# Cache pages in visits of four with seven buffers, and the prompt's causal mask added in VectorE's pass

## The chip, the cores and the metric

The kernel runs on one core of a Trainium2 chip. The metric is the device time of one launch in microseconds, as the median of several runs. The profile shows one such execution, instruction by instruction; its span runs from the first to the last instruction.

## The reference

One inference step of a two-layer decoder: a 512-token prompt and 8 decoding samples of 8 tokens (64 tokens, 576 columns with the prompt's), model width 1024, all in float32. Layer 0 is a gated DeltaNet mixer. Then keys and values are computed once, and layer 1 is a differential attention over them: 8 heads, each with two score components of 64 and values of 128. The prompt attends causally to itself; each sample attends to 1024 cached tokens, in 8 pages of 128 tokens found by a page table, and to its own 8 tokens.

```python
def diff_block(q, k, v, q_pos, k_pos, lam):
    s = jnp.einsum('bqhmd,bkhmd->bhmqk', q, k) * DIFF_DH ** -0.5
    s = jnp.where((k_pos[None, :] <= q_pos[:, None])[None, None, None], s, -jnp.inf)
    p = jax.nn.softmax(s, axis=-1)
    p = p[:, :, 0] - lam * p[:, :, 1]
    return jnp.einsum('bhqk,bkhe->bqhe', p, v)

k_past = cache_k[page_table].reshape(db, past, DIFF_HEADS, 2 * DIFF_DH)
v_past = cache_v[page_table].reshape(db, past, DIFF_HEADS, DIFF_VH)
...
o = rms_norm(o, sub_gain) * (1.0 - lam_init)
o = o * jax.nn.silu(z).reshape(b, L, DIFF_HEADS, DIFF_VH)
return o.reshape(b, L, DIFF_WIDTH) @ w_out
```

## The kernel before

The first part (`phase_a`, to about 640 us) does layer 0. The change lies in the second, `phase_b`. Its order of instructions is not written by hand: a small planner, the class `Second`, runs many generators. Each yields a step: an engine (E is TensorE, A ScalarE, D and S VectorE, P and Q POOL, None a step on no engine), an assumed cost in microseconds, and conditions: results that must be done and rooms (buffers) that must be free. At each turn the planner takes the step that can start first, and of those with the same start the lowest rank. It prices a change of TensorE's tiling itself:

```python
        if mode != self.mode:
            self.cost += 0.2 if mode == (128, 128) else 0.115
```

`pin` then fixes that order on TensorE, ScalarE, VectorE, POOL and SP, so each engine runs its list strictly in order and waits where an input is late. On the chip the waits are by data, not by the planner's clock.

The generators that matter here:

- `weights` and `split_w` load 47 weight sets (128 x 8 x 128, 512 KB each) through two raw buffers on SP's queue. ScalarE casts a set to `whi` (L2018), and POOL, for some sets VectorE, subtracts to get `wlo` in two pieces (L2024). The matrices come in rows of eight sets: the first layer's output projection, then from set 8 queries, from 16 keys, from 24 values, from 32 the gate z, from 40 the output projection. Up to set 23 four buffers turn; from 24 on the room `w2`, with two buffers early and a third (`P.third`) from about 870 us, when the memory of the earlier stage is free. Set 26 has a place of its own.
- `second_projections` (rank 1000, so whatever else can start goes first) multiplies these sets with the hidden state, split in the same way: `run_part` issues three matmuls of 288 columns for each of 8 chunks, 24 for one half of a set. In `out_second`, at the end, four half-tiles of sets 40 and 41 run up to their last chunk before they are finished.
- `Pages.loads` (rank 9) loads the 128 cache pages of 512 KB, in the order keys of samples 0 to 2, then values and keys in turn. It waits for a room `pg` (five buffers), copies the page number on POOL (L2478), reads it into a register on SP (L2481) and issues the load on SP (L2483).
- `Sample2.keys` multiplies the queries with two pages at a time, in the 128x32 tiling (tile `px`); `softmax` follows, and `values` takes two value pages at a time (tile `po`). I call each such group of matmuls a visit. On the chip the pages' buffers are freed as the last matmul on them is done.
- `samples_end` gathers the samples' outputs, normalizes them and multiplies them with the gate; the samples' half of the output projection waits for that.
- `Prompt2.heads` issues the prompt's scores for each head and block of 128 queries (two components in the 64x128 tiling, into rooms `sc`), and then adds the causal mask on the diagonal block by one matmul with the identity for each (bf16, `cmaskb`). `unit` follows with the negated maximum on VectorE (L2714), the exponential on ScalarE (L2718), the combination of the two components on VectorE (L2731), TensorE's transposes into `pt2`, a copy on ScalarE (L2743) and the product with the values (`pv`).

Of the kernel before, what the change touches and what calls it, by code (L numbers as in the profile page):

```python
# [10 lines left out]
F32 = mybir.dt.float32  # L11
# [879 lines left out]
HELD = 4  # L891
EV = 3
CH = 3
PB = 3
# [1100 lines left out]
def weights(W, K, first, n, slot):  # L1995


    for j in range(first, first + n):
        room = "w" if j < 24 else "wx" if j == 26 and EV > 2 else "w2"
        yield None, 0, Room("raw")  # L2000
        rr, = W.took
        raw = K.wraw.tile([128, 8, 128], F32, name="wraw")
        K.nc.sync.dma_start(out=raw[:], in_=K.wall[K.worder[K.wnext + j]].rearrange("p (k m) -> p k m", m=128))
        if j <= 2:
            W.done[("raw", j)] = 0.0, None
        else:
            W.load("S", 1.5, "raw", j)
        W.add(4, split_w(W, K, j, raw, rr, room, slot[room]))


def split_w(W, K, j, raw, rr, room, slot):
    nc = K.nc
    yield "A", act(1024), ("raw", j), Room(room), *((("wa", j - 1),) if j - 1 in W.sets and j > 1 else ())
    took, = W.took
    phi, plo = slot(took[1])
    hi = phi.tile([128, 8, 128], F32R, name="whi")
    lo = plo.tile([128, 8, 128], F32R, name="wlo")
    nc.scalar.copy(out=hi[:], in_=raw[:])  # L2018
    W.sets[j] = hi, lo, took
    W.set("wa", j)  # L2020
    for q in range(0, 8, 4):
        shared = q and HALF[0] <= j < HALF[1]
        yield ("S", dve(512)) if shared else ("P", pool_op(512))
        (nc.vector if shared else nc.gpsimd).tensor_sub(out=lo[:, q:q + 4], in0=raw[:, q:q + 4], in1=hi[:, q:q + 4].bitcast(F32))  # L2024
    W.leave(rr)
    W.set("w", j)
# [320 lines left out]
def second_projections(W, K):  # L2347
# [40 lines left out]
    for i, (m, half) in enumerate(order):  # L2388
        if i < 3:
            bank = early[i][2]  # L2390
            yield from run_part(W, K, m, bank[0], half, (6, 7), conds=heads_in)
        else:
            yield from one(m, m, half, "o", nothing)
            bank = W.done_bank
        if half:
            W.leave(W.sets[m][2])
# [19 lines left out]
    for t, bank in zip(tiles, banks):  # L2416
        W.add(0, t.evac(1, bank))
        W.leave(W.sets[8 + t.h][2])
    yield None, 0, *[("ada", n, "used") for n in range(0, len(KTS2), 2)]
# [16 lines left out]
def tile_row(W, K, tiles, j, kind, conds, first=0):  # L2436
# [6 lines left out]
    for t, half in order:  # L2443
        name = "pp" if kind in "qk" or t.h < EV and kind == "v" else "pq"
        if kind == "v" and t.h == EV and half == 0:
            yield None, 0, ("late",)
        yield from take(W, K, pick(W, "pq", "pt2", "sc", "pv") if kind == "z" and ("pv", 7, 3) in W.done else name)
        bank, = W.out
        yield from run_part(W, K, j + t.h, bank[0], half, range(8), conds=conds[half])
        W.add(0, t.evac(half, bank))  # L2450
        if half:
            W.leave(W.sets[j + t.h][2])
            if j + t.h in (20, 21, 22):
                W.leave(("w2", j + t.h - 20) if j + t.h < 22 else ("wx", 0))
        if t.h == 7:
            W.set(kind + "p", half)


class Pages:


    def __init__(self, W, K):
        self.W, self.K = W, K
        self.tiles = {}
        self.order = [("k", b) for b in range(PB)]
        for b in range(NB):
            self.order += [("v", b)] + ([("k", b + PB)] if b + PB < NB else [])

    def loads(self):
        W, K, P = self.W, self.K, self.W.P  # L2470
        nc = K.nc
        for kind, b in self.order:
            for pg in range(NPG):
                yield "Q", 0.2, Room("pg"), ("ptt",), ("sq", *PAGES_AT)
                i = b * NPG + pg
                t = K.pg.tile([128, 8, 128], F32, name="pg")
                e = t[0:1, 0, 0:1].bitcast(I32)
# [5 lines left out]
                nc.sync.dma_start(out=t[:], in_=cache[bass.ds(r, 1)].rearrange("a p (h t) -> p (a h) t", h=8))  # L2483
                W.load("S", 1.55, kind + "page", i)


class Sample2:
# [5 lines left out]
    def keys(self):  # L2493
# [14 lines left out]
        for half in range(2):  # L2508
            for pair in range(2):
                ids = [b * NPG + 4 * half + 2 * pair + i for i in range(2)]  # L2510
                yield "E", None, *[("kpage", i) for i in ids], *((Room("px"),) if pair == 0 else ())
# [3 lines left out]
                for n, i in enumerate(ids):  # L2515
                    kp, kr = self.G.tiles["k", i]
                    o = 128 * (2 * pair + n)
                    for hh in range(2):
# [64 lines left out]
    def values(self):  # L2583
        W, K, P, b = self.W, self.K, self.W.P, self.b
        nc = K.nc
        for pair in range(4):
            ids = [b * NPG + 2 * pair + i for i in range(2)]
            yield "E", None, *[("vpage", i) for i in ids], *((Room("po"),) if pair == 0 else ())
# [3 lines left out]
            for n, i in enumerate(ids):  # L2592
                vp, vr = self.G.tiles["v", i]
                pg = 2 * pair + n
                for hf in range(2):
# [21 lines left out]
def samples_end(W, K):  # L2617
# [13 lines left out]
    r0, = W.took  # L2631
    sq = K.pg.tile([128, 8, 128], F32, name="pg")[:].rearrange("p a b -> p (a b)")[:, 0:512]
    nc.scalar.activation(out=sq.rearrange("p (h t) -> p h t", t=64), in_=o, func=AF.Square)
# [40 lines left out]
class Prompt2:  # L2674
# [5 lines left out]
    def heads(self):  # L2680
        W, K, P = self.W, self.K, self.W.P
        nc = K.nc
        for h in range(8):
            for qts in (0, 1), (2,), (3,):
# [4 lines left out]
                for qt, pss in units:  # L2689
                    for m in range(2):  # L2690
                        r = slice(64 * m, 64 * m + 64)
                        W.matmul(out=pss[m], lhsT=P.qT[r, h, 128 * qt:128 * qt + 128], rhs=P.kT[r, h, 0:128 * (qt + 1)],
                                 start=(qt == qts[0]), stop=False, tile_position=(64 * m, 0))
                for qt, pss in units:
                    for m in range(2):
                        W.matmul(out=pss[m][:, 128 * qt:128 * qt + 128], lhsT=K.identb, rhs=K.cmaskb, start=False,
                                 stop=(qt == qts[-1]))
                for qt, pss in units:
                    W.add(W.rank - 1, self.unit(h, qt, pss, rooms))

    def unit(self, h, qt, pss, rooms):
# [4 lines left out]
        for m in range(2):  # L2706
# [7 lines left out]
            nc.vector.tensor_reduce(out=mx[:, m:m + 1], in_=pss[m], axis=AX.X, op=ALU.max, negate=True)  # L2714
# [3 lines left out]
            nc.scalar.activation(out=p[:, :w], in_=pss[m], func=AF.Exp, bias=mx[:, m:m + 1],  # L2718
                                 accum_out=ls[:, qt, m:m + 1])
# [69 lines left out]
def out_second(W, K):  # L2789
# [40 lines left out]
    for (m, half), bank in zip(order[:HELD], held):  # L2830
        yield from run_part(W, K, 40 + m, bank[0], half, (7,), conds=conds(half))
        W.add(0, evac(m, half, bank))
        if half:
            W.leave(W.sets[40 + m][2])
    for i, (m, half) in enumerate(order[HELD:]):
# [5 lines left out]
        if half:  # L2841
            W.leave(W.sets[40 + m][2])

# [48 lines left out]
def set_up(W, K, one):  # L2892
# [47 lines left out]
    yield "D", 0.8, ("cm",)  # L2940
    nc.vector.tensor_copy(out=K.identb, in_=K.ident)
    nc.vector.tensor_copy(out=K.cmaskb, in_=cm)
    yield "D", 0.6
# [19 lines left out]
def phase_b(K, ctx, past):  # L2963
# [16 lines left out]
    P.rstd = K.pg.tile([128, 8, 128], F32, name="pg")[:].rearrange("p a b -> p (a b)")[:, 0:NT]  # L2980
    K.identb = first.tile([128, 128], BF16, name="identb")[:]
    K.cmaskb = first.tile([128, 128], BF16, name="cmaskb")[:]
    P.kT = first.tile([128, 8, NT], F32, name="kT")
# [16 lines left out]
    for name, bufs in (("pp", 3), ("pt", 2), ("px", 2), ("po", 1), ("pg", PG), ("scr", SB), ("ch", CH), ("vch", EV), ("tk", 2), ("raw", 2),  # L3000
                       ("w", 4), ("w2", 3), ("wx", 1), ("qs", 2), ("p", PB), ("pTs", 1), ("os", 1), ("C", 2), ("ls", 2), ("mx", 2),
                       ("pq", 1), ("pt2", 1), ("sc", 2), ("pv", 1), ("pm0", PM[0]), ("pm1", PM[1]), ("pts", 1)):
        W.room(name, bufs)
    W.taken["pg"] = W.taken["w"] = 1
    W.taken["w2"], W.taken["wx"] = 3, 1
    W.sets[0] = *K.wq.pop(0), ("w", 0)
    W.done[("w", 0)] = max(0.0, past.done[("w", past.last)][0] - past.free["E"]), None
    own = K.whi, K.wlo
    pages = Pages(W, K)
# [3 lines left out]
    slot = {"w": lambda i: own if i % 4 < 2 else qx, "w2": lambda i: own if i % 3 < 2 else P.third, "wx": lambda i: qx}  # L3013
    W.add(3, weights(W, K, 1, 47, slot))
# [195 lines left out]
```

## Time and profile before

| | |
|---|---|
| median of 3 runs | 1165.18 us (1161.04 to 1165.52) |
| the profiled execution | 1162.21 us |
| its span | 1160.5 us |
| TensorE busy | 1131.4 us, 97% of the span |
| VectorE, ScalarE busy | 690.6 and 692.3 us |
| POOL busy | 437.7 us |
| granted TensorE clock, mean | 0.994 |
| moved by DMA | 239.96 MB, 207 GB/s over the span |

In the profile's rows PE is TensorE, PEld its weight load, DVE VectorE, ACT ScalarE and SPq or POOLq the sequencer of SP or POOL. `px<-pg,qs` names the tile written and those read, `128*32` is TensorE's tiling, L1927 the line in the kernel. All matmuls of the second part go through a helper and have L1927 (transposes L1932), so they are told apart by their tiles. A float32 matmul has two records. The records overlap, since matmuls are pipelined; the time that one takes from TensorE is read from start to start.

### The profile page before, as it was taken

To read this page: it belongs to the slowest core of one execution; us is meant where nothing else is said; L and a number is where in the kernel's file an instruction comes from. 1 tells how busy PE (TensorE), PEld (TensorE's weight loads), DVE (VectorE), ACT (ScalarE), POOL (GpSimd) and SP (SyncE) were. 2 spreads that over 40 slices of the span, in tenths; PEclk is the share of its full clock that TensorE was granted. 3 is DMA by queue.
4 is the path that set the end of the run, shared out by engine and by line. 5 is a ranking of instruction groups with operands and counts; after the bars stand their busy time and mean duration, and the time that the engine had idled before them with its cause. 6 is when DMAs were issued, how large, how long until landed. Compare 5 with 4: busy or idle time off the path is not lost.

```text
span 1160.5 us, 32592 instructions
## 1 busy us (share of the span) xinstructions
PE 1131.4 (97%) x12715; PEld 1039.0 (90%) x12715; DVE 690.6 (60%) x1739; ACT 692.3 (60%) x1901; POOL 437.7 (38%) x752
## 2 busy tenths in 40 slices
PE   8999999999999999999999999999999999999998
PEld 6899998989989998998989999999997887778998
DVE  4677875767877674866743757574424445554342
ACT  3675867777777767676653334775535656555320
POOL 3443434233333333232223431579933232233341
PEclk8999999999999999999999999999999999999999
DMA  9796666757657665676885888222689989898243
GB/s 365 207 230 167 147 193 134 201 146 201 167 153 171 157 199 134 190 204 149 244 248 157 304 274 322 92 74 75 231 290 309 313 310 303 300 320 282 63 137 110
DMA packets 87643, 239.96 MB, mean 207 GB/s; under 512 B 14451, under 2 KB 28659, under 8 KB 87491
## 3 DMA queue, kind: packets, MB, share of 16 engines
q1 hardware_dynamic: 71938, 181.27, 46.0%
q0 software_dynamic: 15552, 56.63, 22.4%
q8 instruction: 100, 1.64, 0.6%
q14 instruction: 53, 0.43, 0.1%
HBM read 212.02 MB, written 25.84 MB: 205 GB/s over the span
## 4 chain that ended last, share of the span: by engine, by line
PE 80%; DMA 6%; ACT 5%; issue 3%; DVE 3%; POOL 2%; SPq 0%; POOLq 0%; ACTq 0%; DVEq 0%
PE pp L271 23%; PE pp L1927 14%; PE pc L271 7%; PE pq L1927 6%; PE px L1927 4%; PE pa L271 3%; PE po L1927 3%; DMA whi<-wall 3%; PE pt L271 3%; PE sc L1927 3%; PE pt L1927 3%; PE pt L1932 3%; PE pv L1927 2%; PE ps L271 2%; PE pt L285 1%
## 5 line engine op out<-in xcount | busy, mean ns | idle before, releaser
L271 PE MATMUL pp<-hlo,whi 128*128 128x288 f32 x592 | 170.7, 310 | 0.0
L271 PE MATMUL pp<-hhi,whi 128*128 128x288 f32 x592 | 162.0, 295 | 0.0
L2024 POOL TENSOR_TENSOR wlo<-wraw,whi 128x512 fp32r<-128x512 f32 x82 | 110.1, 1359 | 113.1 <-ACT whi L2018 104.9
L1927 PE MATMUL pp<-hhi,whi 128*128 128x288 f32 x432 | 133.2, 309 | 0.7 <-DVE x L1826 0.7
L1927 PE MATMUL pp<-hlo,whi 128*128 128x288 f32 x432 | 127.3, 295 | 0.0
L1927 PE MATMUL pp<-hhi,wlo 128*128 128x288 f32 x432 | 125.8, 295 | 0.0
L271 PE MATMUL pp<-hhi,wraw 128*128 128x288 f32 x576 | 124.1, 299 | 0.0
L271 PEld LDWEIGHTS pp<-hlo,whi 128*128 128x128 f32 x592 | 111.6, 189 | 1.8 <-issue 1.4
L271 PEld LDWEIGHTS pp<-hhi,whi 128*128 128x128 f32 x592 | 111.7, 189 | 0.4
L271 PE MATMUL pp<-hhi,wlo 128*128 128x288 f32 x592 | 104.1, 304 | 0.0
L271 PEld LDWEIGHTS pp<-hhi,wraw 128*128 128x128 f32 x576 | 94.4, 189 | 1.0 <-issue 0.4
L1131 DVE SCALAR_TENSOR_TENSOR y<-u,vec,y 128x600 f32<-128x600 f32 x96 | 80.9, 842 | 10.8 <-ACT y L1128 10.2
L1927 PEld LDWEIGHTS pp<-hhi,whi 128*128 128x128 f32 x432 | 81.5, 189 | 5.2 <-issue 4.7
L271 PEld LDWEIGHTS pp<-hhi,wlo 128*128 128x128 f32 x592 | 85.1, 190 | 0.8 <-issue 0.2
L2478 POOL COPY pg<-ptt 1x1 int32<-1x1 int32 x128 | 27.5, 222 | 154.0 <-PE px L1927 67.8
L271 PE MATMUL pp<-hlo,wraw 128*128 128x288 f32 x288 | 84.7, 316 | 0.2 <-DVE hlo L1852 0.2
L1927 PEld LDWEIGHTS pp<-hlo,whi 128*128 128x128 f32 x432 | 81.6, 189 | 0.0
L1927 PEld LDWEIGHTS pp<-hhi,wlo 128*128 128x128 f32 x432 | 80.9, 189 | 0.0
L923 POOL DMA_DIRECT2D wlo<-wall x36 | 32.2, 895 | 122.4 <-ACT wlo L918 80.9
L2018 ACT CAST whi<-wraw 128x1024 fp32r<-128x1024 f32 x47 | 49.0, 1047 | 40.0 <-DMA wraw<-wall 20.1
L1927 PE MATMUL pq<-hhi,whi 128*128 128x288 f32 x192 | 61.9, 322 | 1.6 <-DVE x L2230 1.0
L1927 PE MATMUL pq<-hhi,wlo 128*128 128x288 f32 x192 | 56.7, 295 | 0.0
(483 smaller groups left out, 3135.5 us busy)
## 6 DMA issues: line engine op xcount, KB each, us to landing
pg<-ck SPq DMA_DIRECT2D x64, 512.0 KB, 5.1
pg<-cv SPq DMA_DIRECT2D x64, 512.0 KB, 4.9
wraw<-wall SPq DMA_DIRECT2D x49, 512.0 KB, 4.3
wraw<-wall POOLq DMA_DIRECT2D x36, 512.0 KB, 5.9
whi<-wall POOLq DMA_DIRECT2D x36, 512.0 KB, 5.8
wlo<-wall POOLq DMA_DIRECT2D x36, 512.0 KB, 5.7
araw<-ada SPq DMA_DIRECT2D x24, 512.0 KB, 4.3
araw<-ada SPq DMA_DIRECT2D x8, 1024.0 KB, 13.2
```

What stands on the lines that cost most here:

```text
L271: return self.K.nc.tensor.matmul(**kw)
L285: return self.K.nc.tensor.transpose(**kw)
L923: K.nc.gpsimd.dma_start(out=lo[:], in_=src, accum_op=ALU.add)
L1131: nc.vector.scalar_tensor_tensor(out=y[:, :YW], in0=u[:, j:j + YW], scalar=cw[j], in1=y[:, :YW], op0=ALU.mult, op1=ALU.add)
L1927: return self.K.nc.tensor.matmul(**kw)
L1932: return self.K.nc.tensor.transpose(**kw)
L2018: nc.scalar.copy(out=hi[:], in_=raw[:])
L2024: (nc.vector if shared else nc.gpsimd).tensor_sub(out=lo[:, q:q + 4], in0=raw[:, q:q + 4], in1=hi[:, q:q + 4].bitcast(F32))
L2478: nc.gpsimd.tensor_copy(out=e, in_=P.ptt[0:1, i:i + 1])
```

## The change

1. Visits of four pages instead of two (`BURST`), for the keys from the fourth sample on and for all values.
2. Two more page buffers (`K.pg2`, `MORE`), seven in all, from the point at which the earlier stage's memory is free.
3. The third late weight set is gone; `w2` has two buffers throughout. Weight set 40 is split into two page buffers (`OVER`), once all page loads are issued.
4. The mask's matmuls are gone. VectorE's reduction becomes a pass that adds the mask to the scores, negates them, writes them back to PSUM and gives their minimum; ScalarE's exponential takes them with a scale of -1. The mask's constant is now 512 wide, zeros before the diagonal block, and an identity in bf16 is no longer made.

```diff
+BURST = 4
+MORE = 2
+OVER = 40,
...
-        room = "w" if j < 24 else "wx" if j == 26 and EV > 2 else "w2"
+        room = "w" if j < 24 else "wx" if j == 26 and EV > 2 else "pg" if j in OVER else "w2"
...
-    yield "A", act(1024), ("raw", j), Room(room), *((("wa", j - 1),) if j - 1 in W.sets and j > 1 else ())
+    yield ("A", act(1024), ("raw", j), *((Room(room),) if slot else (Room(room), Room(room), ("loads",))),
+           *((("wa", j - 1),) if j - 1 in W.sets and j > 1 else ()))
...
+        hi, lo = (W.pages.tile(r)[:].bitcast(F32R) for r in W.took)
...
+    def tile(self, room):
+        n = room[1] - self.grown
+        pool = self.K.pg2 if n >= 0 and n % (PG + MORE) < MORE else self.K.pg
+        return pool.tile([128, 8, 128], F32, name="pg")
...
+        W.set("loads")
...
-            for pair in range(2):
-                ids = [b * NPG + 4 * half + 2 * pair + i for i in range(2)]
+            many = BURST if b >= PB else 2
+            for pair in range(4 // many):
+                ids = [b * NPG + 4 * half + many * pair + i for i in range(many)]
...
-        for pair in range(4):
-            ids = [b * NPG + 2 * pair + i for i in range(2)]
+        for pair in range(NPG // BURST):
+            ids = [b * NPG + BURST * pair + i for i in range(BURST)]
...
-                                 start=(qt == qts[0]), stop=False, tile_position=(64 * m, 0))
-                for qt, pss in units:
-                    for m in range(2):
-                        W.matmul(out=pss[m][:, 128 * qt:128 * qt + 128], lhsT=K.identb, rhs=K.cmaskb, start=False,
-                                 stop=(qt == qts[-1]))
+                                 start=(qt == qts[0]), stop=(qt == qts[-1]), tile_position=(64 * m, 0))
...
-            nc.vector.tensor_reduce(out=mx[:, m:m + 1], in_=pss[m], axis=AX.X, op=ALU.max, negate=True)
+            nc.vector.tensor_tensor_reduce(out=pss[m], in0=pss[m], in1=K.cmaskb[:, 512 - w:512], scale=-1.0, scalar=-NEG * 2,
+                                           op0=ALU.add, op1=ALU.min, accum_out=mx[:, m:m + 1])
...
-            nc.scalar.activation(out=p[:, :w], in_=pss[m], func=AF.Exp, bias=mx[:, m:m + 1],
+            nc.scalar.activation(out=p[:, :w], in_=pss[m], func=AF.Exp, bias=mx[:, m:m + 1], scale=-1.0,
...
-    nc.vector.tensor_copy(out=K.identb, in_=K.ident)
-    nc.vector.tensor_copy(out=K.cmaskb, in_=cm)
+    nc.vector.memset(K.cmaskb[:, 0:384], 0.0)
+    nc.vector.tensor_copy(out=K.cmaskb[:, 384:512], in_=cm)
...
-                       ("w", 4), ("w2", 3), ("wx", 1), ("qs", 2), ("p", PB), ("pTs", 1), ("os", 1), ("C", 2), ("ls", 2), ("mx", 2),
+                       ("w", 4), ("w2", 2), ("wx", 1), ("qs", 2), ("p", PB), ("pTs", 1), ("os", 1), ("C", 2), ("ls", 2), ("mx", 2),
...
-    P.third = [pool(n, 1) for n in ("bwh", "bwl")]
-    W.done[("late",)] = W.left["w2", 2] = W.now, None
+    K.pg2 = pool("bpg2", MORE)
+    pages.grown = W.taken["pg"]
+    W.bufs["pg"] += MORE
+    W.done[("late",)] = W.now, None
```

More of the change, by code (lines that the diff above doesn't have):

```diff
@@ L2007, in weights @@
             W.load("S", 1.5, "raw", j)
-        W.add(4, split_w(W, K, j, raw, rr, room, slot[room]))
+        W.add(4, split_w(W, K, j, raw, rr, room, slot.get(room)))
 def split_w(W, K, j, raw, rr, room, slot):
     nc = K.nc
-    yield "A", act(1024), ("raw", j), Room(room), *((("wa", j - 1),) if j - 1 in W.sets and j > 1 else ())
[L2014 to L2017, printed above, removed]
+    yield ("A", act(1024), ("raw", j), *((Room(room),) if slot else (Room(room), Room(room), ("loads",))),
+           *((("wa", j - 1),) if j - 1 in W.sets and j > 1 else ()))
+    took = W.took
+    if slot:
+        phi, plo = slot(took[0][1])
+        hi = phi.tile([128, 8, 128], F32R, name="whi")
+        lo = plo.tile([128, 8, 128], F32R, name="wlo")
+    else:
+        hi, lo = (W.pages.tile(r)[:].bitcast(F32R) for r in W.took)
     nc.scalar.copy(out=hi[:], in_=raw[:])
@@ L2395, in second_projections @@
         if half:
-            W.leave(W.sets[m][2])
+            W.leave(*W.sets[m][2])
         yield None, 0, ("xl", half, m)
@@ L2417, in second_projections @@
         W.add(0, t.evac(1, bank))
-        W.leave(W.sets[8 + t.h][2])
+        W.leave(*W.sets[8 + t.h][2])
     yield None, 0, *[("ada", n, "used") for n in range(0, len(KTS2), 2)]
@@ L2451, in tile_row @@
         if half:
-            W.leave(W.sets[j + t.h][2])
+            W.leave(*W.sets[j + t.h][2])
             if j + t.h in (20, 21, 22):
@@ L2463, in __init__ @@
         self.W, self.K = W, K
-        self.tiles = {}
+        self.tiles, self.grown = {}, math.inf
         self.order = [("k", b) for b in range(PB)]
@@ L2475, in loads @@
                 i = b * NPG + pg
-                t = K.pg.tile([128, 8, 128], F32, name="pg")
+                t = self.tile(W.took[0])
                 e = t[0:1, 0, 0:1].bitcast(I32)
@@ L2516, in keys @@
                     kp, kr = self.G.tiles["k", i]
-                    o = 128 * (2 * pair + n)
+                    o = 128 * (many * pair + n)
                     for hh in range(2):
@@ L2593, in values @@
                 vp, vr = self.G.tiles["v", i]
-                pg = 2 * pair + n
+                pg = BURST * pair + n
                 for hf in range(2):
@@ L2631, in samples_end @@
     r0, = W.took
-    sq = K.pg.tile([128, 8, 128], F32, name="pg")[:].rearrange("p a b -> p (a b)")[:, 0:512]
+    sq = W.pages.tile(r0)[:].rearrange("p a b -> p (a b)")[:, 0:512]
     nc.scalar.activation(out=sq.rearrange("p (h t) -> p h t", t=64), in_=o, func=AF.Square)
@@ L2833, in out_second @@
         if half:
-            W.leave(W.sets[40 + m][2])
+            W.leave(*W.sets[40 + m][2])
     for i, (m, half) in enumerate(order[HELD:]):
@@ L2841, in out_second @@
         if half:
-            W.leave(W.sets[40 + m][2])
+            W.leave(*W.sets[40 + m][2])
 def ada_later_loads(W, K, kts, bufs, ns, at):
@@ L2980, in phase_b @@
     P.rstd = K.pg.tile([128, 8, 128], F32, name="pg")[:].rearrange("p a b -> p (a b)")[:, 0:NT]
-    K.identb = first.tile([128, 128], BF16, name="identb")[:]
-    K.cmaskb = first.tile([128, 128], BF16, name="cmaskb")[:]
+    K.cmaskb = first.tile([128, 512], BF16, name="cmaskb")[:]
     P.kT = first.tile([128, 8, NT], F32, name="kT")
@@ L3004, in phase_b @@
     W.taken["pg"] = W.taken["w"] = 1
-    W.taken["w2"], W.taken["wx"] = 3, 1
-    W.sets[0] = *K.wq.pop(0), ("w", 0)
+    W.taken["w2"], W.taken["wx"] = 2, 1
+    W.sets[0] = *K.wq.pop(0), [("w", 0)]
     W.done[("w", 0)] = max(0.0, past.done[("w", past.last)][0] - past.free["E"]), None
     own = K.whi, K.wlo
-    pages = Pages(W, K)
+    pages = W.pages = Pages(W, K)
     samples = [Sample2(W, K, pages, b) for b in range(NB)]
@@ L3012, in phase_b @@
     W.add(7, set_up(W, K, one))
-    slot = {"w": lambda i: own if i % 4 < 2 else qx, "w2": lambda i: own if i % 3 < 2 else P.third, "wx": lambda i: qx}
+    slot = {"w": lambda i: own if i % 4 < 2 else qx, "w2": lambda i: own, "wx": lambda i: qx}
     W.add(3, weights(W, K, 1, 47, slot))
```

## The prediction

> **What bounds the kernel now.** I read the page's busy shares and the chain first, then the stage table, then TensorE's own order of instructions around the page visits. The first fence is from the page: busy times, and the chain of work that ended last.
>
> ```profile
> PE 1131.4 (97%) x12715; PEld 1039.0 (90%) x12715; DVE 690.6 (60%) x1739; ACT 692.3 (60%) x1901; POOL 437.7 (38%) x752
> PE 80%; DMA 6%; ACT 5%; issue 3%; DVE 3%; POOL 2%; SPq 0%; POOLq 0%; ACTq 0%; DVEq 0%
> ```
>
> TensorE is busy for 97% of the span and carries 80% of the chain. The stages of the second half (start:end, length, busy time of each engine, clock, DMA share, GB/s) show the stretch in which the change works (cache visits and prompt attention, 870 to 1060), the rest of the gate projection behind it, and the output projection.
>
> ```profile
> 870.00:1060.00 190.00, 186.27 (x2617) 150.85 (x2616) 99.10 (x251) 111.01 (x322) 59.26 (x148) 1.00 0.89 306
> 1080.00:1110.00 30.00, 27.99 (x212) 27.32 (x211) 15.70 (x30) 12.14 (x27) 12.13 (x9) 1.00 0.28 82
> 1110.00:1161.00 51.00, 46.63 (x352) 46.39 (x351) 13.56 (x35) 5.86 (x7) 12.65 (x10) 1.00 0.38 118
> ```
>
> From 870 to 1060 TensorE idles 3.7 us of 190. VectorE is busy for 99 of them; the DMA engines are at 0.89, so they come next. Whenever pages or scores are missing, TensorE takes the value and gate projections (rank 1000), so time taken off its list comes off the end, as long as the pages still arrive in time. The page loads themselves wait for buffers that TensorE frees, and TensorE hardly waits for pages (waits, and who waited for the page tile):
>
> ```profile
> POOL pg L2478 <- PE px L1927: 60.8, 34, 5.7
> POOL pg L2478 <- PE po L1927: 55.4, 40, 5.8
> PE px L1927 <- DMA pg<-ck: 1.4, 1, 1.4
> PE po L1927 <- POOL pg L2478: 0.8, 2, 0.4
> PE po L1927 <- DMA pg<-cv: 0.2, 1, 0.2
> ```
>
> **Part 1, visits of four.** The page tile's rows, then TensorE's timeline (start, duration, instruction) around two visits:
>
> ```profile
> L1927 PE MATMUL px<-pg,qs x1024: 269/273/298, 813.4 to 1028.8; 128*32 128x128 f32 x171
> L1927 PE MATMUL po<-pg,pTs x1024: 269/273/298, 872.3 to 1076.5; 128*32 128x128 f32 x171
> ...
> 909.55 0.64 PE L1927 MATMUL po<-pg,pTs 128*32 128x128 f32 x16
> ...
> 1050.72 0.30 PE L1927 MATMUL pq<-hlo,whi 128*128 128x288 f32 x1
> 1050.86 0.29 PE L1927 MATMUL pq<-hhi,wlo 128*128 128x288 f32 x1
> 1051.08 1.08 PE L1927 MATMUL po<-pg,pTs 128*32 128x128 f32 x32
> 1052.09 0.40 PE L1927 MATMUL pq<-hhi,whi 128*128 128x288 f32 x1
> ```
>
> A page is 8 matmuls in the program (one a head) and 16 records, so a visit of two pages is 32 records, and 2048 records are 64 visits; the timeline shows all 64 apart, with other work between. Sixteen records more make a visit 1.08 - 0.64 = 0.44 us longer, 0.0275 us a record, so the arithmetic of a visit is 32 x 0.0275 = 0.88 us. From its start to the next projection's start pass 1.01 us: 0.13 us go in leaving the 128x32 tiling. Into it, 0.22 us pass from the projection's last matmul, where two projection matmuls are 0.13 to 0.14 apart: 0.09 us. A visit thus costs 0.22 us beside its arithmetic. After the change the keys of the first three samples (read before the seven buffers exist) keep 3 x 4 = 12 visits, the other five have 5 x 2 = 10, the values 8 x 2 = 16: 38 instead of 64. Saved: 26 x 0.22 = 5.7 us, all on TensorE. The bounds: 0, if the new order puts the freed switches elsewhere; 26 x 0.315 = 8.2 us by the planner's own prices for the two switches (0.115 and 0.2 in `change`). I take 5.7, since the 64 visits stand apart in this trace and the gaps are its own.
>
> **Part 2, the mask's matmuls.** 64 of them (bf16, 128 columns) go, in 24 groups of two or four:
>
> ```profile
> L1927 PE MATMUL sc<-cmaskb,identb x64: 218/220/232, 876.3 to 1054.4; 128*128 128x128 bf16 x64
> ...
> 906.13 0.29 PE L1927 MATMUL sc<-cmaskb,identb 128*128 128x128 bf16 x2
> 906.35 1.08 PE L1927 MATMUL px<-pg,qs 128*32 128x128 f32 x32
> ...
> 1048.46 0.29 PE L1927 MATMUL sc<-cmaskb,identb 128*128 128x128 bf16 x2
> 1048.58 0.39 PE L1927 MATMUL px<-C,sp 128*128 128x64 f32 x2
> ```
>
> Their 0.22 us overlap. By starts a pair takes 0.12 us before work in the full tiling and 0.22 before a page visit, where 0.09 is the visit's own entry and stays: 0.06 us each. 64 x 0.06 = 3.8 us; with the full 0.22 at the groups that stand before a visit it would be about 4.8. The change from the scores' 64-row tiling to the next one is paid in both kernels. I take 4.0.
>
> **Part 3, the mask in VectorE's pass.** 64 reductions become 64 passes with a second operand, a write back to PSUM and a minimum. The nearest rows are the reduction itself, a two-operand pass of the same widths (L2731), and ScalarE's read of its accumulator:
>
> ```profile
> L2714 DVE TENSOR_REDUCE mx<-sc x64: 279/484/693, 876.7 to 1056.4; 128x1 f32<-128x128 f32 x16, 128x1 f32<-128x256 f32 x16, 128x1 f32<-128x384 f32 x16, 128x1 f32<-128x512 f32 x16
> L2731 DVE SCALAR_TENSOR_TENSOR pm<-pm,cf,pm x32: 350/552/1705, 880.9 to 1059.1; 128x128 f32<-128x128 f32 x8, 128x256 f32<-128x256 f32 x8, 128x384 f32<-128x384 f32 x8, 128x512 f32<-128x512 f32 x8
> L2718 ACT ACTIVATION_READ_ACCUMULATOR pm<-sc,mx x64: 189/202/224, 877.6 to 1058.5; 128x1 f32 x64
> L1932 PEld LDWEIGHTS pt<-con_ident,pm 128*128 128x128 f32 x80 | 9.3, 143 | 2.9 <-issue 1.8 <-ACT vs L2336 0.5 <-DVE pm L2731 0.3
> ```
>
> The second operand costs 0.07 us by the medians (552 against 484 ns); a separate read of the minimum would be up to 0.2 us more. So a pass takes 0 to 0.27 us longer, VectorE 0 to 17 us in a stage where it is idle for 91 of 190. What a late maximum delays is the unit's exponential, its VectorE combination and then TensorE's transposes of pm; behind these wait the score rooms and all that stands later in TensorE's order. Two passes a unit make that 0 to 0.54 us, and TensorE waited for pm only 0.3 us in all. So between 0 and 32 x 0.54 = 17 us; I take 1.0, near the row of 0.3. ScalarE's exponential only gets a scale. On this the Trainium skill speaks against the change: "VectorE: DVE Perf Modes", section "Two Vector instructions with no wait between them", counts an op that writes out an accumulator as two instructions; no VectorE row here shows such an op. By it a pass would take the upper value, and the sum would be -7.7 as below; without it a pass would take the lower ones, and the sum would be about -8.2.
>
> **Part 4, buffers and weight sets.** The rows: POOL's and ScalarE's work on one of the last weight sets, the chain's last two halves of a set, the page loads' issues after 864 us and their time to land, and TensorE's first matmuls of the output projection.
>
> ```profile
> 1131.23 1.05 ACT L2018 CAST whi<-wraw 128x1024 fp32r<-128x1024 f32 x1 [4.04 <-PE pv L1927]
> 1132.35 2.54 POOL L2024 TENSOR_TENSOR wlo<-wraw,whi 128x512 fp32r<-128x512 f32 x2 [2.55 <-ACT whi L2018]
> ...
> 1150.26 3.17 PE pt L1927 x24
> 1153.43 3.21 PE pv L1927 x24
> ...
> L2483 SPq DMA_DIRECT2D pg<-cv x64: 337/338/418, 864.1 to 1069.6; - x64
> L2483 SPq DMA_DIRECT2D pg<-ck x40: 337/338/683, 884.1 to 1022.8; - x40
> DMA to landing us min/median/max: 3.4/4.9/7.4
> ...
> 1104.26 0.40 PE L1927 MATMUL pq<-hhi,whi 128*128 128x288 f32 x1 [1.05 <-DVE x L2230]
> 1108.39 0.40 PE L1927 MATMUL px<-hlo,whi 128*128 128x288 f32 x1 [0.96 <-DVE hlo L2670]
> ```
>
> With seven buffers and visits of four, three loads are still under way when a visit may begin, as with five and two (7 - 4 = 5 - 2), and pages are 205.5/103 = 2.0 us apart, so three cover the 4.9 us of a landing. Four are freed together and reloaded through POOL's copy (behind the weights' subtractions there) and SP's register load and issue; the samples' next visit waits for them, and other units of TensorE fill in. The late third weight set goes, so a set is refilled only when the one two before it is done. Refilling takes 1134.9 - 1131.2 = 3.7 us; the other set holds two halves of 3.2 us. So it is covered even at the dense end, with 2.7 us to spare; if that cover were gone, about ten sets would cost up to 3.7 us each. Set 40 (first of the output projection, wanted at 1104 us) is split into two page buffers once all loads are out (1069.6 us). It stands ahead of set 41's cast in ScalarE's order, which waits for the end of a gate-projection set, three microseconds before 1104, anyway. Cost nothing. The mask's wider constant replaces a copy by a fill in the set-up, 200 us before its use: nothing. The waits for a fourth page and the new order of everything after 870: the stalls there are 5.7 us now (3.7 to 1060, 2.0 after 1080). They can go to 0, or grow by half a page's spacing, 1.0 us, at each of 26 larger visits: 26 us. I take +1.0, near the 2.4 us that 64 visits wait now.
>
> **Sum.** -5.7 - 4.0 + 1.0 + 1.0 = -7.7 us: span 1152.8. The profiled execution took 1162.2, 1.7 more than its span; so 1154.5 on its own time. It lies 3.0 below the median of the three runs (1165.2; 1161.0 to 1165.5). A change of 0.5%, about 6 us, is what a measurement can tell from none. I say 1155, between the two scales and nearer the profile's.
>
> **Rivals.** (a) *The loads become the bound.* If visits of four slow the loading by 5% of its 205 us (864 to 1069.6), the last visit ends 10 us later while the projections that cover it end 10 us earlier.
>
> ```profile
> 1075.70 1.08 PE L1927 MATMUL po<-pg,pTs 128*32 128x128 f32 x32
> 1087.83 1.05 PE L1927 MATMUL px<-con_ident,rny 128*128 128x128 f32 x8
> GB/s 297 326 260 253 328 388 290 239 362 329 274 332 389 256 267 287 395 308 305 290 297 286 320 349 292 277 374 226 330 276 278 311 335 318 367 347 157 290 287 317
> ```
>
> From the last visit to the last matmul ahead of the samples' normalized output are 12.1 us, and I estimate 4 more to the gated value, ready near 1092; the samples' half of the output projection wants it at 1108. The 16 us of cover would be eaten by 10 + 10: 4 us exposed. Gain 3 to 4 us and some waits: 1160. For it: DMA at 0.89 already. Against it: POOL's copies wait 116 us for buffers, so the visits pace the loads rather than the reverse, and the third row (GB/s in slices of 5 us, 864 to 1070) has slices of 362 to 395 beside a mean of 306. The Trainium skill ("DMA: Bandwidth & Descriptors", Specifications) gives about 358 GB/s as a core's limit from HBM; by it the loads could go an estimated 15% faster at most, enough for this change too, though the trace's short slices exceed it.
>
> (b) *TensorE stands at the visits* (slower). It executes in order; if the last of four pages lands late at each of the 26 larger visits by w, the time is 1155 + 26 w. From w = 0.3 us the gain is gone; at 1.0 us (half the pages' spacing) it is 1181. For it: the fourth load of a group is issued after the release. Against: 2.4 us of such waits over 64 visits now.
>
> (c) *The stalls go as well.* Most of the 5.7 us falls away with two more buffers: 1150.
>
> **How the numbers follow.** Forecast 0.56 (its own range 1150 to 1159), (a) 0.19, (b) 0.12, (c) 0.13. Faster by over 0.5% (below 1159.4): most of the forecast and (c), 0.68; within: (a) and an edge, 0.20; slower: (b), 0.12. The range runs from (c)'s far end to (a) and the light end of (b), w = 0.4: 1147 to 1165.
>
> **What would show it.** 38 groups of page matmuls, mostly x64, 1.01 + 0.88 = 1.9 us from start to the next work; no cmaskb rows; TensorE busy 9 to 10 us less; the mx rows at 0.5 to 0.75 us; pages' last visit near 1070; output projection from about 1095. I am wrong if TensorE's waits for pg or pm exceed 8 us, if the last visit moves beyond 1085, or if sets 41 to 47 make TensorE wait.

## The result and the profile after

The changed kernel takes 1151.6 us (median of 4 runs, 1150.5 to 1152.6) against 1163.1 for the kernel before on the same chip: a ratio of 0.9895, 95% interval 0.9867 to 0.9924. A second measurement with the last experiments gave 0.9934 (0.9909 to 0.9960). The profiled execution took 1150.7 us with a span of 1149.0, 11.5 us less than before.

Not all of these 11.5 us can be put down to the change. The first visit to a cache page starts at 813.4 us before and at 811.2 after. Over the fourteen profiles here that start lies at 811.8 to 819.5 in the five with three late weight sets and at 809.6 to 814.1 in the nine with two; the ranges overlap, and whether the change has a part in it is not shown. So I read each profile from its first page visit to the start of its last matmul, and call this the second half: 342.9 us before, 333.6 after, and 333.9 in a second profile of the changed kernel: 9.2 us less on average. Two kernels were profiled twice, and their second halves agree within 0.3 and 1.0 us; for the others it is one execution.

The page after: busy times and the chain that ended last.

```profile
PE 1118.5 (97%) x12651; PEld 1036.0 (90%) x12651; DVE 694.6 (60%) x1803; ACT 693.9 (60%) x1901; POOL 439.4 (38%) x752
PE 78%; ACT 7%; DVE 5%; DMA 5%; issue 3%; POOL 2%; SPq 1%; POOLq 0%; ACTq 0%; DVEq 0%
```

TensorE has 12.9 us less to do and is as full as before; ScalarE and VectorE have gained a share of the chain. The stages after (columns as in the prediction):

```profile
870.00:1060.00 190.00, 188.47 (x2635) 161.90 (x2636) 105.80 (x320) 112.58 (x326) 56.27 (x143) 1.00 0.89 306
1060.00:1110.00 50.00, 46.00 (x445) 44.22 (x438) 21.77 (x42) 18.25 (x43) 15.94 (x15) 0.93 0.39 124
...
1088.00:1092.00 4.00, 2.26 (x19) 2.03 (x17) 3.97 (x6) 2.32 (x9) 2.71 (x2) 1.00 0.36 99
1092.00:1096.00 4.00, 1.74 (x6) 1.42 (x6) 3.12 (x9) 0.90 (x2) 0.00 (x0) 0.56 0.38 122
1096.00:1100.00 4.00, 4.00 (x21) 4.00 (x21) 0.00 (x0) 0.00 (x0) 0.00 (x0) 0.59 0.00 0
1100.00:1104.00 4.00, 4.00 (x33) 4.00 (x32) 0.00 (x0) 0.00 (x0) 0.00 (x0) 1.00 0.02 4
```

In the page stage TensorE now idles 1.5 us of 190 instead of 3.7, and the DMA engines move exactly what they moved before, 306 GB/s at a share of 0.89. The loads did not speed up. What is new lies at 1090 us: a hole, and two slices in which the granted clock is 0.56 and 0.59 on average. Read in slices of 1 us, it is 1.00 up to 1092, 0.72 in the next, 0.50 in each from 1093 to 1099, 0.86 in the one behind and then 1.00 again: half clock for nearly 7 us, of which 1.5 fall into the wait itself. TensorE's waits from 860 us on, and the page tile's last visits and value loads:

```profile
PE px L1930 <- ACT hhi L2682: 3.7, 1, 3.7
PE pt L1935 <- ACT vch L2247: 0.5, 1, 0.5
PE pq L1930 <- ACT vch L2247: 0.4, 2, 0.2
PE po L1930 <- POOL pg L2490: 0.4, 1, 0.4
PE px L1930 <- DVE hlo L2684: 0.3, 1, 0.3
```

```profile
L1930 PE MATMUL po<-pg,pTs x1024: 269/273/298, 874.8 to 1077.5; 128*32 128x128 f32 x171
...
L2495 SPq DMA_DIRECT2D pg<-cv x64: 337/338/749, 862.7 to 1069.9; - x64
```

All waits for pages are down to 0.4 us (2.4 before), but 3.7 us stand at the samples' gate: the samples' half of the output projection (`px<-hhi`) waits for ScalarE's cast of the gated output. TensorE's timeline shows a visit of four, and then the gate:

```profile
906.59 0.29 PE L1930 MATMUL pq<-hlo,whi 128*128 128x288 f32 x1
906.72 0.29 PE L1930 MATMUL pq<-hhi,wlo 128*128 128x288 f32 x1
906.94 1.96 PE L1930 MATMUL po<-pg,pTs 128*32 128x128 f32 x64
908.83 0.33 PE L1935 MATMUL pt<-con_ident,vch 128*128 128x128 f32 x1
...
1086.42 0.30 PE L1930 MATMUL pq<-hhi,pg 128*128 128x288 f32 x1
...
1089.97 0.29 PE L1930 MATMUL pq<-hhi,pg 128*128 128x288 f32 x1
1093.95 0.61 PE L1930 MATMUL px<-hhi,pg 128*128 128x288 f32 x1 [3.68 <-ACT hhi L2682]
1094.87 0.61 PE L1930 MATMUL px<-hlo,pg 128*128 128x288 f32 x1 [0.32 <-DVE hlo L2684]
1095.28 0.68 PE L1930 MATMUL px<-hhi,pg 128*128 128x288 f32 x2
1095.76 0.44 PE L1930 MATMUL px<-hlo,pg 128*128 128x288 f32 x1
```

The visit takes 1.89 us to the next work, the same 0.22 us of entering and leaving as a visit of two. The output projection (`pq<-hhi,pg`, set 40 in page buffers) starts at 1086.4 instead of 1104.3; its first half-tile is issued by 1090.3, and the samples are not ready (the second half-tile takes the last 224 columns of the prompt and the 64 of the samples). Behind the wait the matmuls are 0.24 us apart instead of 0.13, for 18 of them, some 2 us more. What the gate waits for is on VectorE; its timeline, POOL's beside it, and the splits' row:

```profile
1087.61 0.69 DVE L2677 TENSOR_TENSOR qT<-x,qT 128x512 f32<-128x512 f32 x1
1088.34 2.73 DVE L2684 TENSOR_TENSOR hlo<-qT,hhi 128x224 fp32r<-128x224 f32 x2
1091.00 0.74 DVE L2666 SCALAR_TENSOR_TENSOR qT<-px,sg,qT 128x512 f32<-128x512 f32 x1
1091.66 0.98 DVE L2684 TENSOR_TENSOR hlo<-qT,hhi 128x224 fp32r<-128x224 f32 x3
1092.56 0.68 DVE L2677 TENSOR_TENSOR qT<-x,qT 128x512 f32<-128x512 f32 x1
...
1088.11 2.71 POOL L2031 TENSOR_TENSOR wlo<-wraw,whi 128x512 fp32r<-128x512 f32 x2 [1.14 <-ACT whi L2025]
...
L2684 DVE TENSOR_TENSOR hlo<-qT,hhi x11: 374/379/1461, 1084.2 to 1094.7; 128x224 fp32r<-128x224 f32 x8, 128x288 fp32r<-128x288 f32 x2, 128x512 fp32r<-128x512 f32 x1
```

TensorE's last matmuls for the samples' normalization start at 1088.0 and take 1.05 us, but VectorE normalizes (L2666) only at 1091.0. Two splits of the prompt's gated output (`hlo`) stand ahead in its order and take 2.7 us together, where a split of this width takes 0.38 (the median) elsewhere; POOL's subtraction of a weight set runs in just these 2.7 us.

VectorE's pass is two instructions:

```profile
L2724 DVE CUSTOM_DVE_ANT_0 sc<-sc,cmaskb x64: 282/506/732, 873.0 to 1056.7; 128x128 f32<-128x128 f32 x16, 128x256 f32<-128x256 f32 x16, 128x384 f32<-128x384 f32 x16, 128x512 f32<-128x512 f32 x16
L2724 DVE DVE_READ_ACCUMULATOR2_ANT mx<- x64: 82/141/144, 873.3 to 1057.4; 128x1 f32 x64
```

That is 0.51 + 0.14 us against 0.48. The Trainium skill ("VectorE: DVE Perf Modes", "Two Vector instructions with no wait between them") counts an op that also writes out its accumulator as two instructions: the trace agrees, with a read of 0.141 us.

### The profile page after: what moved, and what is told of

Its sections match the earlier page's. It is cut to its first block, busy times and chain, and to the rows that moved or that the text cites. A ratio compares the mean times of both kernels' runs of the same rounds, so it can differ in the third digit from the quotient of the medians.

```text
span 1149.0 us, 32501 instructions
## 1 busy us (share of the span) xinstructions
PE 1118.5 (97%) x12651; PEld 1036.0 (90%) x12651; DVE 694.6 (60%) x1803; ACT 693.9 (60%) x1901; POOL 439.4 (38%) x752
## 4 chain that ended last, share of the span: by engine, by line
PE 78%; ACT 7%; DVE 5%; DMA 5%; issue 3%; POOL 2%; SPq 1%; POOLq 0%; ACTq 0%; DVEq 0%
PE pp L271 24%; PE pp L1930 12%; PE pc L271 7%; PE pq L1930 7%; PE px L1930 4%; PE po L1930 3%; PE pa L271 3%; PE sc L1930 3%; PE pt L1935 3%; PE pt L271 3%; PE pt L1930 2%; PE pv L1930 2%; PE ps L271 2%; DMA whi<-wall 2%; PE pt L285 1%
## 5 line engine op out<-in xcount | busy, mean ns | idle before, releaser
L1930 PE MATMUL pq<-hhi,whi 128*128 128x288 f32 x200 | 65.0, 325 | 0.6 <-ACT vch L2247 0.4
L1930 PE MATMUL pq<-hlo,whi 128*128 128x288 f32 x200 | 58.9, 295 | 0.0
```

Source lines behind the costliest of these rows:

```text
L1930: return self.K.nc.tensor.matmul(**kw)
```

## The experiments

The times below are ratios to the kernel before, with 95% intervals. "Second half" is the stretch defined above, and "last visit" the start of the last visit after the first one, both in us; each value is from one profiled execution.

| kernel | ratio | second half | last visit |
|---|---|---|---|
| before | 1 | 342.9 | 262.3 |
| before, reordered end | 0.9994 (0.9973 to 1.0014) | 341.8 | 262.3 |
| VectorE's pass, matmuls kept | 1.0005 (0.9988 to 1.0022) | 341.9 | 261.2 |
| mask alone | 0.9987 (0.9968 to 1.0006) | 342.3 | 264.7 |
| mask, reordered end | 0.9942 (0.9924 to 0.9961) | 335.8 | 262.1 |
| buffers alone | 0.9959 (0.9940 to 0.9978) | 338.7 | 224.9 |
| buffers and visits | 0.9942 (0.9919 to 0.9966) | 335.2 | 259.1 |
| buffers and mask | 0.9912 (0.9889 to 0.9934) | 335.1 | 232.9 |
| the same, reordered end | 0.9946 (0.9928 to 0.9964) | 334.4 | 233.4 |
| the change | 0.9895, 0.9934 | 333.6, 333.9 | 264.5, 264.7 |
| the change, reordered end | 0.9873 (0.9841 to 0.9904), 0.9880 (0.9853 to 0.9907) | 329.3, 328.4 | 265.0, 264.0 |
| the change, five buffers | 1.0361 (1.0330 to 1.0392) | 387.9 | 313.0 |

**The mask alone.** The kernel before with the fourth point of the change and nothing else.

> The kernel before with the mask's part of the change alone (no bf16 matmuls, the mask added in VectorE's pass). Theory: TensorE loses 4.75 us of work by starts (24 groups), and the projections behind the last cache visit still cover the samples' path (16 us of cover, some 5 eaten), so the span goes from 1160.5 to about 1156, a ratio near 0.996. Rival 1 (the gain of the whole change comes from the buffers and visits, the mask's matmuls were hidden in gaps): ratio 1.000 within 0.15%. Rival 2 (the pass of 0.65 us instead of 0.49 makes TensorE wait for the maxima): TensorE's waits for pm grow by several us and the ratio is above 1.000.

It came to 0.9987, an interval that holds no change: the number of rival 1, for another reason. The mask's 4.7 us did leave TensorE's list, and counted from the first visit the samples' half-tile starts 3.3 us earlier (290.4 instead of 293.7). From there to the end it takes 2.7 us more. Waits from 1040 us on, two slices with the clock behind them, and VectorE and POOL ahead of the wait:

```profile
PE px L1927 <- DVE hlo L2670: 2.2, 1, 2.2
```

```profile
1104.00:1108.00 4.00, 1.81 (x9) 1.55 (x9) 4.00 (x8) 1.65 (x6) 2.00 (x2) 0.82 0.72 217
1108.00:1112.00 4.00, 4.00 (x25) 4.00 (x25) 1.72 (x5) 0.71 (x2) 0.00 (x0) 0.76 0.19 75
```

```profile
1094.58 0.75 DVE L2652 SCALAR_TENSOR_TENSOR qT<-px,sg,qT 128x512 f32<-128x512 f32 x1 [2.31 <-PE px L1927]
...
1102.28 0.46 DVE L2230 SCALAR_TENSOR_TENSOR x<-scr,pt 128x288 f32<-128x288 f32 x1 [0.56 <-ACT scr L2228]
1102.77 0.69 DVE L2663 TENSOR_TENSOR qT<-x,qT 128x512 f32<-128x512 f32 x1
1103.49 3.96 DVE L2670 TENSOR_TENSOR hlo<-qT,hhi 128x224 fp32r<-128x224 f32 x5
...
1103.26 2.74 POOL L2024 TENSOR_TENSOR wlo<-wraw,whi 128x512 fp32r<-128x512 f32 x2 [0.38 <-ACT whi L2018]
```

2.2 us of wait, and 25 matmuls in 4 us where 32 go at full clock. This wait is not the visits' doing: the samples' output was normalized at 1094.6 (L2652) and then stood until the last gate projection came out (1102.7). From there to the wait's end pass 4.2 us, as in the kernel before (1104.2 to 1108.4): the gate's product, two slow prompt splits (1.4 us each) beside POOL's subtraction, and the samples' split (the last three within the row x5). Before, TensorE had its two waits there, 1.05 and 0.96 us, apart; now they are one of 2.2, and the clock falls behind it.

**Buffers alone.** Seven page buffers, two late weight sets and set 40 in page buffers; visits of two, the mask by matmuls.

```diff
-BURST = 4
+BURST = 2
(and the mask's part as before)
```

> The kernel before with seven page buffers late, two late weight sets and set 40 in page buffers, visits of two and the mask by matmuls. Theory: TensorE's work is the same and it hardly waited for pages, so 1160 plus or minus 2 us of span; the last page visit may move forward by a few us and the end does not follow. Rival (the loads held the kernel back, and two more buffers free them): last page visit 8 us or more earlier and the time 5 us or more down, a ratio below 0.996.

The rival was nearer: 0.9959, at the edge of what it asked for. The page tile's row:

```profile
L1930 PE MATMUL po<-pg,pTs x1024: 269/273/297, 872.4 to 1038.4; 128*32 128x128 f32 x171
```

The last visit is 37 us earlier, counted from the first. But TensorE had waited for pages only 2.4 us, and gained 4.2 in the second half. By starts and from the first visit on, TensorE's own work took 2.5 us less, of this 1.8 in the projections (70 stretches instead of 80: with the attention done early, they run on with fewer breaks), and its waits fell by 1.7 us.

**Buffers and visits.** The change without the mask's part.

> The changed kernel with the mask by matmuls again: visits of four, seven buffers, two late sets. Theory: 26 visits fewer at 0.22 us, 5.7 us off TensorE, all of it at the end, span about 1154, ratio near 0.995; with the mask alone it then adds up to more than the change gave, because there 4 us of wait at the samples' gate and some 2.4 us of half clock behind it are lost. Rival (the visits only move waits about): ratio within 0.15% of that of the buffers alone.

0.9942, which by the ratios alone cannot be told from the buffers alone; the second half is 3.5 us under theirs, where 5.7 had been expected. Of the 2.2 us missing, 1.1 are waits (5.2 instead of 4.1) and 1.0 are the projections, in 79 stretches again. The loads gave back their lead: the last visit is at 259.1 again, 34 us later than with visits of two.

**The reordered end.** The changed kernel, in which the first half-tiles of the output projection are both prompt halves and then both samples' halves.

```diff
-    order = [(m, half) for m in range(8) for half in range(2)]
+    order = [(0, 0), (1, 0), (0, 1), (1, 1)] + [(m, half) for m in range(2, 8) for half in range(2)]
-    names = ["pq", "px", "px", "po", "sc", "sc", "pt2", "pv"]
+    names = ["pq", "sc", "px", "px", "po", "sc", "pt2", "pv"]
```

> The changed kernel with the output projection's first four half-tiles in the order: prompt half of tile 0, prompt half of tile 1, then the samples' halves of both (and the PSUM banks in an order to fit). Theory: the wait of 3.7 us for the samples' gate at 1090 is filled with 2.8 us of the second prompt half, so at most 1 us of wait stays and the clock is not halved behind it (0.56 to 0.59 from 1092 to 1100 in the changed kernel): span 1149.0 minus 2.8 minus up to 2.4, about 1144 to 1146, ratio to the kernel before near 0.987. Rival (the end is set by something behind the gate, such as the last two weight sets or the transfers of the output): no more than 1 us gained, 1148 or above.

0.9873: faster than the kernel before; beside the changed kernel's 0.9895 the intervals still overlap. The second half is 4.3 us shorter than in the changed kernel. TensorE's waits at the gate:

```profile
PE px L1930 <- ACT hhi L2682: 0.9, 1, 0.9
PE px L1930 <- DVE hlo L2684: 0.5, 1, 0.5
```

and its timeline there, again 0.13 us a matmul right behind the wait:

```profile
1095.06 0.40 PE L1930 MATMUL px<-hhi,pg 128*128 128x288 f32 x1 [0.93 <-ACT hhi L2682]
1095.99 0.41 PE L1930 MATMUL px<-hlo,pg 128*128 128x288 f32 x1 [0.53 <-DVE hlo L2684]
1096.23 0.43 PE L1930 MATMUL px<-hhi,pg 128*128 128x288 f32 x2
1096.49 0.29 PE L1930 MATMUL px<-hlo,pg 128*128 128x288 f32 x1
```

**Buffers and mask, visits of two.** The changed kernel with `BURST = 2`.

> The changed kernel with visits of two (seven buffers, two late sets, the mask in VectorE's pass). Theory: the mask's matmuls are worth their 4.75 us wherever the samples' gate is covered. With visits of two and seven buffers the last page visit was at 1038 us and the gate had some 40 us of cover, so against the buffers alone (span 1155.5) the mask now takes off 4 to 5 us: span about 1151, ratio to before near 0.992. Rival (moving the mask gains nothing by itself: VectorE's longer pass gives back what TensorE saves): span 1155 to 1156, ratio as with the buffers alone.

0.9912 against 0.9959 for the buffers alone, 3.6 us in the second half and 5.5 by the ratios. TensorE's waits at the end are the same in both (1.05 and 0.97 us), and so the mask pays.

**Mask with the reordered end.** The mask alone with the same two lines changed.

> The mask's part alone, with the output projection's first half-tiles reordered (two prompt halves, then two samples' halves). Theory: the mask alone gained nothing because TensorE waited 2.2 us for the samples' gate at 1105 and then ran 3 us at half clock; 2.8 us of prompt work put there take most of both away, so 3 to 4 us come off: span 1156 to 1157. Rival (the 4.75 us were given back before the gate, by VectorE's pass and by waits for pages): the gate's wait goes, and the end stays within 1.5 us of 1160.3.

0.9942, second half 335.8, that is 6.4 us under the mask alone; the profile has no wait at the gate at all (its span is 1159.5 only because its first visit came at 819.5). So most of the mask's work had been given back at the gate and behind it.

**VectorE's pass by itself.** The kernel before with the pass; the 64 matmuls stay and add zeros.

```diff
-                        W.matmul(... lhsT=K.identb, rhs=K.cmaskb, ...)
+                        W.matmul(... lhsT=K.cmaskb[:, 384:512], rhs=K.cmaskb[:, 0:128], ...)
```

> The kernel before with the mask added in VectorE's pass and the 64 matmuls kept (they add zeros: the mask's constant times a block of zeros). It costs the pass by itself: 0.51 + 0.14 us instead of 0.49. Theory: TensorE's list is as before, its waits for pm grow by 1 us at most, span 1160 to 1162. Rival (the pass delays the units): 1164 or more, waits for pm or for the pts copy of several us.

1.0005, second half 1 us under before: here the pass costs nothing that can be measured. TensorE's waits from 1040 us on are the old ones, none of them for pm:

```profile
PE pq L1927 <- DVE x L2230: 1.0, 1, 1.0
PE px L1927 <- DVE hlo L2670: 1.0, 1, 1.0
PE po L1927 <- DMA pg<-cv: 0.5, 1, 0.5
```

**Five buffers.** The changed kernel with `MORE = 0`, so that four of five buffers belong to the visit.

> The changed kernel with five page buffers (visits of four, two late sets, the mask in the pass). One load instead of three is under way when a visit may begin. Theory: loads are paced by the visits' releases; a cycle of four pages then lasts about the landing of four loads issued together, 9 to 10 us instead of 8, so the last visit moves from 1076 to 1100 or later, the gate is exposed by 15 us or more beyond the 3.7, and the time ends above the kernel before: 1165 to 1185. Rival (the DMA engines and not the buffers set the pace of the loads): the last visit stays within 5 us and so does the time, 1149 to 1155.

1.0361: the theory's direction, and further than its range (second half 387.9). The stage, and TensorE's waits for pages from 1040 us on:

```profile
870.00:1060.00 190.00, 183.56 (x2188) 157.04 (x2186) 107.97 (x316) 107.47 (x320) 53.63 (x117) 1.00 0.69 231
```

```profile
PE po L1930 <- DMA pg<-cv: 15.3, 14, 2.7
PE px L1930 <- DMA pg<-ck: 4.4, 3, 2.5
```

The loads fall to 231 GB/s, the projections run out while pages are still to come, and then TensorE stands at the visits, with a clock of 0.73 from 1060 to 1110.

**The controls.** The kernel before with the reordered end; the changed kernel with visits of two and the reordered end; and both changed kernels once more.

> The kernel before with the output projection's first half-tiles reordered and nothing else: the control for the two reordered kernels. Before waited 1.05 and 0.96 us at the end of the gate projection and at the samples' gate. Theory: at most these 2 us come off, a ratio of 0.998 to 1.000; the mask with the same order (0.9942) is then worth 4 to 6 us. Rival (the order by itself is worth what the mask with it gained): ratio near 0.994.

> The changed kernel with visits of two and the reordered output projection. Against the reordered kernel with visits of four it shows what the visits are worth where the samples' gate costs nothing in either. Theory: 26 switches into and out of the tiling at 0.22 us, so this kernel is 5 to 6 us slower than the reordered one with visits of four, ratio to before near 0.991. Rival (the visits of four bring no more than the 2 us that they brought in the kernels with the old order): within 2 us of it, ratio 0.9885 or less.

> The changed kernel with the reordered output projection, once more, beside its two controls on one chip. Theory: the ratio is 0.987 as before, 2 to 3 us under the changed kernel. Rival (the first measurement flattered it): 0.989 or more, the same as the changed kernel.

> The changed kernel itself on the same chip as the reordered ones, for a narrower interval. Theory: ratio 0.9895 as before, with one wait of 3 to 4 us at the samples' gate and a clock near 0.57 behind it. Rival (wait and clock are an accident of one execution): no wait above 1 us there in this profile.

The order by itself is worth 1.2 us in the second half and nothing measurable in the ratio (0.9994). Visits of two with it take 334.4, visits of four 329.3 and 328.4: 5.5 us, where the old order showed 1.5; the ratios, 0.9946 against 0.9873 and 0.9880, lie apart as well. The reordered kernel repeats at 0.9880. The changed kernel came to 0.9934 this time, clear of it; its profile has the same wait of 3.7 us, and the clock is at 0.50 for nearly 7 us again (1094.1 to 1100.9). The rival, an accident of one execution, is out.

## Why the prediction was right, and where its steps were not

The time is right: 1155 was forecast on a mixed scale and 1154.5 on the profile's own, 1151.6 was measured; the sum said 7.7 us, the second half shows 9.2. That it came so close is in part luck. With the gate covered in both kernels the change takes off 12.9 us (341.8 against 328.9), 5.2 more than the sum; the gate, which the sum left out, took 3.7 of them back. The terms:

- *Visits of four, 5.7 us.* Right where the gate is covered: 5.5 (reordered end, two against four), and a visit of four has the same 0.22 us about it. With the mask by matmuls and the old order it was 3.5, since waits and broken-up projections took some of it.
- *The mask's matmuls, 4.0 us.* Somewhat low. By starts all 4.7 us went, as the upper value had it; in the second half, with the reordered end, the mask is worth 341.8 - 335.8 = 6.0, its pass included. Of the 1.2 us more, 0.7 are waits that went (4.6 to 3.9 us after the first visit); the rest is not traced.
- *VectorE's pass, +1.0.* Too much for the changed kernel: none of TensorE's waits there is for pm, nor in the pass by itself. A pass is 0.16 us longer, inside the bounds. With visits of two, seven buffers and the pass, though, TensorE waits 1.2 us for pm (L2742), in two waits; the buffers alone, without the pass, show none. Whether the pass causes it was not tried; if it does, the price of 1.0 holds there.
- *Buffers and new order, +1.0.* Wrong in sign. Seven buffers and two late sets are worth 4.2 us alone, and 1.5 beside the mask with the gate covered (335.8 against 334.4). In the changed kernel no weight set made TensorE wait.
- *Left out: the gate, +4.9.* This is the step that failed. Rival (a) saw that the cover of the samples' path would be eaten, but made it hang on slower loads, and set 10 us of saved work against 16 us of cover. Counted from the first visit, the output projection starts at 275.2 us instead of 290.9: TensorE's work up to there fell by 12.4 us, and its waits, 4.9 us before, to 1.6. The last visit is 2.2 us later, and the path behind the normalization takes 5.9 us (1088.0 to 1093.9), not the 4 that I estimated. So 15.7 + 2.2 + 1.9 = 19.8 us stood against 16: 3.8 us exposed, and 3.7 measured. The 1.9 us are VectorE's: it normalizes 3.0 us after TensorE's matmuls for it start, where in the kernel before it was 1.1. In the changed kernel the gate projection ends just ahead, and so the prompt's splits, two of them at 1.4 us instead of 0.38, have come to stand in the samples' path. Nor was the old cover of 16 us the whole gate: the 2.0 us that TensorE waited at this end before hung on the last gate projection, as in the mask alone. With the slow clock behind it the gate costs 4.9 us, which the reordered end gets back (333.8 to 328.9 on average); it was worth 1.2 in the kernel before. The loads were punctual; the saved waits and the splits were what I had left out.

Taken one after another behind a reordered end, the mask is worth 6.0 us, the buffers 1.5 and the visits 5.5. Whether they add up in another order was not tried in full; with the old end they do not: there the mask is worth 0.7 us alone, 3.6 beside the buffers and 1.4 beside buffers and visits.

The claim "three loads are under way, as with five and two" was right by the count of buffers, and it was the key to the loads: with five under way behind a visit (seven buffers, visits of two) the last visit is at 225 to 233 us, with three at 259 to 265, with one at 313. Visits of four thus gave up the lead that two more buffers had bought the loads, and bought fewer switches with it, to TensorE's advantage.

## What to carry to other kernels

On an engine that is nearly full, set against the cover of the next serial chain all that moves its start, waits that go included, and not the saved work alone; then look for other work to stand in the hole (two swapped half-tiles brought nearly as much here as the mask: 4.9 us and 6.0). Test each part also with the next wait removed: the mask showed nothing alone (0.9987) and 6 us so. The pace of paged loads goes by the buffers that are under way behind a visit, so a larger visit needs as many more buffers as it adds pages. Look also at what stands ahead of the chain on the other engines' lists: here two slow VectorE splits.

## What the runs showed of the hardware

TensorE's granted clock can fall behind a short wait. At the samples' gate, waits of about 1 us (before, and the reordered end) left it at 1.00; one of 2.2 us was followed by slices of 0.82 and 0.76, and 3.7 us, in both profiles of the changed kernel, by nearly 7 us at 0.50, with matmuls 0.24 us apart instead of 0.13. In these three waits the clock fell 1.8 to 2.6 us after the wait began. A wait of 3.7 us thus cost nearly 6 us. The length of the wait alone does not settle it: in the run of the pass by itself, 2.4 us of wait for tile pp at 662 us left the clock at 1.00 in every slice of 4 us up to 672, while in the second profile of the reordered change 1.45 us at 457 was followed by 0.72 and 0.85. What decides was not tried.

A split on VectorE (128x224) that ran beside POOL's subtraction of a weight set took 1.4 us instead of 0.38, in the kernel before, in the mask alone and in the change alike. That POOL is the cause is likely from the times, but no run here moved it.

A longer VectorE pass with an accumulator read (0.65 us instead of 0.48, 64 times) had no price in the kernel before or in the changed one, where VectorE idles for 84 of 190 us.
